# Windowed attention in an encoder layer: the second score product on all 128 rows of the array, and the products with v in alternating column halves

## The chip, the cores and the metric

The kernel runs on one core of a Trainium2 chip. The metric is device time in microseconds (us) of one execution of the whole kernel. PE is TensorE (PEld its weight loads), DVE is VectorE, ACT is ScalarE, POOL is GpSimd, SP is SyncE, which issues the DMAs.

## The reference, cut to what matters

The program is one hybrid encoder layer of 1024 tokens and 1024 features: a gated linear recurrence and a windowed attention side by side, a cross-attention into a memory, a gated MLP, each with its norm and residual. The change lies in the windowed attention alone: 8 query heads of 64 features share 2 key/value heads, and a token sees keys at a distance of at most 128. In blocks of 128 queries against up to three blocks of keys:

```python
    s = jnp.einsum('bnqhgd,bnkhd->bnhgqk', qb, kb).astype(jnp.float32) * (ATT_HEAD_DIM ** -0.5)
...
    s = jnp.where(valid[None, :, None, None], s, -jnp.inf)
    sk = sink.astype(jnp.float32).reshape(ATT_KV_HEADS, ATT_GROUP)[None, None, :, :, None, None]
    m = jnp.maximum(jnp.max(s, axis=-1, keepdims=True), sk)
    p = jnp.exp(s - m)
    p = p / (jnp.sum(p, axis=-1, keepdims=True) + jnp.exp(sk - m))
    o = jnp.einsum('bnhgqk,bnkhd->bnqhgd', p.astype(v.dtype), vb)
```

## The kernel before, in words

All engines work from instruction streams that are fixed when the program is built; each engine takes its own stream in order. A scheduler sorts the streams at build time, so that work of different parts is interleaved on PE: while the attention runs, the last chunks of the gate projections (`gate_chunk`, matmuls of L103 into `gate_ps`, 128x512 each) stand between its pieces.

Matrix products in full precision are made from a high and a low part of each operand (`_h`/`_l`, type float32r). For the scores the two parts of q are stacked: a tile `qs[h]` of 128 partitions holds the high part of head h in one half of the partitions and its low part in the other half (odd heads the other way round). `kh[g]` holds the high part of k in both halves, `kl[g]` its low part in both halves (`stacked`, L824 and after; the tiles come by DMA through two `stage` tiles, ACT writes the high parts and DVE the low ones).

The attention is a loop over 8 tiles `i` of 128 tokens and 2 groups `g` of 4 heads: 16 blocks, in the order (0,0), (0,1), (1,0) and so on. A block has two or three key tiles `ks` (two at both ends). Per block:

1. Scores, for each of the 4 heads: two matmuls into one PSUM bank `as` (three such banks): L863 multiplies the whole `qs` with `kh`, over all 128 rows of the array (128x384, or 128x256 at the ends); L865 multiplies the high half of `qs`, 64 rows, with the same half of `kl`.
2. DVE adds the band and takes the row maximum in one pass (L868, result `sm`), negates it (`nm`, L166), and ACT takes the exponentials with their sums (L879). DVE adds the sink's term and inverts (L881, L882), and scales the four heads (L166, `sm<-sm,den`).
3. PE transposes `sm` in pieces of 128x128, four heads into a bank `pt` (L889; two such banks); the middle key tile's bank is copied to `pT` by DVE (L891), the others by ACT (L893).
4. Products with v (L897): `po`, one bank, has 128 partitions, the first 64 for two of the heads (`par` 0) and the last 64 for the other two (`par` 1). The stationary operand is 64 columns wide, so that a product uses one half of the array's columns. In float32 one product is two matmul instructions in the trace. ACT copies `po` to `att` (L901).

The pool `pT` has two buffers, `sm` three, `ao` one. After the loop the attention's result is split (L914, L915) and multiplied with w_br (L103, `y`).

Of the kernel before, what the change touches and what calls it, by code (L numbers as in the profile page):

```python
# [52 lines left out]
def encoder_layer(ctx, tc, x, mem, positions, vecs, fin, sink, w_in, w_br, w_out, w_mq, w_mk, w_mv,  # L53
                  w_mo, w_up, w_down, ident_in, masks_in, band_in, invf_in, out):
    nc = tc.nc
# [39 lines left out]
    def proj_f(ps, w, act, kts=range(KT), koff=0, halves=(0, 1), width=512):  # L95
        """ps[c, tok] = w[k, c]^T act[k, tok] with weights stationary; act(kt, half) -> (hi, lo)."""
        wh, wl = w
        kts = list(kts)
        for n_, hf in enumerate(halves):
            n = 0  # L100
            for wx, ai in ((wh, 0), (wh, 1), (wl, 0)):
                for kt in kts:
                    nc.tensor.matmul(  # L103
                        ps[:, n_ * width:(n_ + 1) * width],
                        lhsT=wx[:, (kt + koff) * P:(kt + koff + 1) * P],
                        rhs=act(kt, hf)[ai],
                        start=(n == 0),
                        stop=(n == 3 * len(kts) - 1),
                    )
                    n += 1  # L110

# [7 lines left out]
    def hi_lo_cols(xs, k2, gcol, ps, hi, lo, w):  # L119
        """Feature chunks 2 k2, 2 k2 + 1 of the tiles xs, transposed, times the gain, as hi and lo."""  # L120
        for a in range(2):
            kt = 2 * k2 + a
            for j, t in enumerate(xs):
                nc.tensor.transpose(ps[:, a, j * P:(j + 1) * P], t[:, kt * P:(kt + 1) * P], ident)
        for a in range(2):
            kt = 2 * k2 + a
            g = vec[:, gcol + kt:gcol + kt + 1]
            nc.scalar.activation(hi[:, a, :], ps[:, a, :w], AF.Copy, scale=g)
            nc.vector.scalar_tensor_tensor(out=lo[:, a, :], in0=ps[:, a, :w], scalar=g,
                                           in1=hi[:, a, :].bitcast(F32),  # L130
                                           op0=ALU.mult, op1=ALU.subtract)

    def norm_half(src, gcol, xs_pool, name, alloc, hf, per=4):
        """Tiles src(hf * per ..) of [128, 1024] -> feature-major (hi, lo) lists of [128, 2, per * 128]."""
        xs = []
        for i in range(hf * per, (hf + 1) * per):
            t = src(i)
            s = xs_pool.tile([P, D], F32, tag="xs", name=f"{name}_xs{i}")
            ss = xs_pool.tile([P, 1], F32, tag="xss", name=f"{name}_ss{i}")
            rs = xs_pool.tile([P, 1], F32, tag="xrs", name=f"{name}_rs{i}")  # L140
            norm_stats(t, s, rs, ss)
            nc.vector.tensor_scalar(out=s, in0=t, scalar1=rs, scalar2=None, op0=ALU.mult)
            xs.append(s)
        w = per * P
        his, los = [], []
        for k2 in range(KT // 2):
            ps = work_psum(f"{name}_tp{hf}_{k2}")
            hi = alloc(f"{name}_h{hf}_{k2}", w)
            lo = alloc(f"{name}_l{hf}_{k2}", w)
            hi_lo_cols(xs, k2, gcol, ps, hi, lo, w)  # L150
            his.append(hi)
            los.append(lo)
        return his, los
# [17 lines left out]
    # With A the weights of two column chunks by halves of K, and B the normed input by halves of K and  # L171
    # of the tokens, the seven products are
    #   M1 = A11 B11, M2 = A12 B21, M3 = S4 B22, M4 = A22 T4, M5 = S1 T1, M6 = S2 T2, M7 = S3 T3.
# [21 lines left out]
    class Operand:  # L195
        """Half of the features by half of the tokens, as hi and lo."""
# [16 lines left out]
    class Strassen:  # L213
        """w_d: weights by column chunks; ts: the eight token tiles, which the norm overwrites; gcol: gains;
        tp: 12 tiles of operands; wq: weight sums; bf: four tiles of the norm's own."""
# [21 lines left out]
        def cols(self, hf, k2, dst):  # L237
            """Feature chunks 2 k2, 2 k2 + 1, transposed, times the gain."""
            for a in range(2):
                kt = 2 * k2 + a  # L240
                ps = self.bank(f"{self.nm}_tp{hf}{kt}")
                for j in range(4):
                    nc.tensor.transpose(ps[:, j * P:(j + 1) * P],
                                        self.ts[4 * hf + j][:, kt * P:(kt + 1) * P], ident)
                g = self.gcol + kt
                nc.scalar.activation(dst[:, a, :], ps, AF.Copy, scale=vec[:, g:g + 1])
# [9 lines left out]
        def half1(self, save12=None):  # L256
            """In steps, so that other work can come between."""
            nm, bf, ts = self.nm, self.bf, self.ts
# [48 lines left out]
        def work(self, tag, name, bufs, width=512):  # L307
            """The first chunks work in the tiles that the norm leaves behind, the others in a pool there."""
            if self.fp is None:
                n = self.used[tag] = self.used.get(tag, -1) + 1  # L310
                return self.left[tag][n % len(self.left[tag])]
            return self.fp.tile([P, width], F32, tag=tag, name=name, bufs=bufs)

        def pair(self, c, name, put):
            """put(row, half, in0, in1): the product of chunk c + row and token half is in0 + in1 (or in0)."""
# [37 lines left out]
        def into(self, outs, tag, names, bufs):  # L353
            """A put that writes the products to tiles of its own."""
            def put(r, hf, a, b):
                if r not in outs:
                    outs[r] = self.work(tag, names[r], bufs, S)
                o = outs[r][:, hf * 512:(hf + 1) * 512]
                if b is None:
                    nc.scalar.copy(o, a)  # L360
                else:
                    add(o, a, b)
            return put

    # ================= token mixing =================
# [19 lines left out]
    # The first chunks' products are plain float32 ones, whose operands need no splitting.  # L385
    w_first, n_plain = [], 2
    for i in range(NT):
        if i < n_plain:
            w = npool.tile([P, 1024], F32, tag="n", name=f"wk{i}")
# [6 lines left out]
    # The memory's norm: its gains go into the operand, its row scales into the products.  # L396
# [73 lines left out]
    # forget-gate bounds: f = fs * tanh(z / 2) + fb  # L470
# [132 lines left out]
    # The weights of the output and the down-projection, in the same form with the even and the odd chunks as  # L603
    # the halves of K; their sums by halves of the columns: T1 T3 T4 T2.
# [47 lines left out]
    with ExitStack() as gla:  # L652
# [10 lines left out]
        def gla_head(h, finish_last):  # L663
# [25 lines left out]
            # same-token terms  # L689
# [34 lines left out]
            # states between tiles  # L724
# [41 lines left out]
            # per-head RMSNorm, output gate  # L766
# [56 lines left out]
    # Stacked operands: a head's q is [hi; lo] (odd heads [lo; hi]) against [k_hi; k_hi], plus hi with k_lo.  # L823
# [24 lines left out]
    for i in range(NT):  # L848
# [4 lines left out]
        for g in range(2):  # L853
# [3 lines left out]
            for pr in range(2):  # L857
                for a in range(2):
                    ps = one_bank(f"as{u}_{pr}", "as", 3, 512)
                    h = 4 * g + 2 * pr + a  # L860
                    rows = HA if h % 2 == 0 else HB
# [3 lines left out]
                    nc.tensor.matmul(ps[:, :nk], lhsT=qs[h][rows, tok], rhs=kl[g][rows, kr],  # L865
# [29 lines left out]
            for par in range(2):  # L895
                for a, j in enumerate(ks):
# [33 lines left out]
    # Left operands of the output projection, by halves of the tokens.  # L930
# [49 lines left out]
    def out_proj(w_d, tag, act, hf, psum4, emit, nk=KT):  # L980
        """Half the tokens times w, by column halves, as the weights arrive: ps[tok, c] = act^T w."""
# [25 lines left out]
    def token_product(name, nk, left, right, banks, first, put, tail, hook=None):  # L1007
        """A product of a left operand (tokens) and a right one (columns) of nk chunks each, in four banks."""
# [69 lines left out]
    # ================= memory cross-attention =================  # L1078
# [8 lines left out]
    def hl(name, tag, bufs, src, scale=None):  # L1087
        """Exact high and low parts of [128, 1024] src (times a power of two)."""
# [90 lines left out]
    # ================= channel mixing =================  # L1179
# [27 lines left out]
    # The left operands, by halves of the tokens: A11 S3 A12 A22 S1 S2 S4.  # L1207
# [53 lines left out]
    def emit_out(i, part):  # L1261
        """Column half part of the residual is complete; the row is when part ends it."""
# [122 lines left out]
```

## Time and profile before

| | |
|---|---|
| Runs of the kernel before | 1803.36, 1806.0, 1807.61 us; median 1806.0 us |
| Profiled execution, from first to last instruction | 1803.6 us (no other time of it is listed) |
| Its PE busy | 1763.9 us (98%) |
| Its DVE, ACT busy | 1195.2 us (66%), 756.5 us (42%) |
| Granted clock of PE, mean | 0.998 of full speed |
| The attention's loop, first score matmul to last product | about 588 to 730 us of the span |

The page shows one execution. Busy times of PE contain modelled ends: a matmul counts as busy until its last result is out, while the next one has long begun, so a full row of "busy" doesn't say that PE is at its peak. Starts are measured; the distance from one start to the next is what an instruction costs the engine. In the chain of waits, a piece's time is its share of the way to the end.

### The profile page before, as it was taken

The page shows a single profiled execution, that of the slowest core. Times are in us where ns is not written, and L with a number is a line of the kernel's source. Part 1 is how long each engine was busy: PE and PEld are TensorE (multiplying, and loading weights), DVE is VectorE, ACT ScalarE, POOL GpSimd, SP SyncE. Part 2 cuts the span into 40 slices and gives each one's busy share as a digit, 9 for nine tenths or more (in the row PEclk, how much of TensorE's full clock was granted, in tenths as well). Part 3 has the DMA queues.
Part 4 walks back from the last instruction along what each step waited for, and adds up shares of the span by engine and source line. Part 5 has one row for each costly group of instructions (what it writes and reads, how often), then busy time and mean ns, then how long its engine had stood idle before and what let it go on. Part 6 is the DMA issues. An engine that isn't in the chain of part 4 may idle for free.

```text
span 1803.6 us, 21596 instructions
## 1 busy us (share of the span) xinstructions
PE 1763.9 (98%) x8372; PEld 1419.8 (79%) x8372; DVE 1195.2 (66%) x1692; ACT 756.5 (42%) x1128; POOL 33.9 (2%) x45
## 2 busy tenths in 40 slices
PE   8999999999999999999999999999999999999998
PEld 7678878888888755788778887878888888788886
DVE  5877765488884576676577454788676677656544
ACT  6643333333232455432344334544433344425335
POOL 1000000000000000000000000000000000000001
PEclk9999999999999999999999999999999999999999
DMA  8375652622213511245267213322223322486663
GB/s 293 130 245 184 208 182 99 257 76 106 94 47 121 164 36 47 94 143 203 88 248 264 70 47 117 117 88 100 99 88 131 109 88 100 153 295 221 206 191 135
DMA packets 85207, 256.37 MB, mean 142 GB/s; under 512 B 8912, under 2 KB 9296, under 8 KB 85104
## 3 DMA queue, kind: packets, MB, share of 16 engines
q1 hardware_dynamic: 85104, 254.99, 41.4%
q8 instruction: 66, 1.08, 0.2%
q14 instruction: 37, 0.30, 0.1%
HBM read 182.73 MB, written 71.57 MB: 141 GB/s over the span
## 4 chain that ended last, share of the span: by engine, by line
PE 77%; DVE 10%; DMA 7%; issue 2%; ACT 2%; POOL 1%; SPq 0%; POOLq 0%; ACTq 0%; DVEq 0%
PE gate_ps L103 6%; PE dnX L1026 5%; PE y L103 5%; PE mq L993 4%; PE xq_ps L103 3%; PE dnZ L1026 3%; PE moX L1026 2%; PE sc L710 2%; PE ao L897 2%; DMA hr<-hid_d 2%; PE moZ L1026 1%; PE xo L1157 1%; PE as L865 1%; PE pt L889 1%; PE xs L1131 1%
## 5 line engine op out<-in xcount | busy, mean ns | idle before, releaser
L103 PE MATMUL gate_ps<-n1B,wh 128*128 128x512 f32 x512 | 135.6, 401 | 0.0
L92 DVE TENSOR_TENSOR wl<-wr,wh 128x1024 fp32r<-128x1024 f32 x70 | 85.4, 1223 | 54.8 <-ACT wh L91 24.1
L91 ACT CAST wh<-wr 128x1024 fp32r<-128x1024 f32 x70 | 73.6, 1052 | 103.1 <-PE xq_ps L103 22.0
L103 PEld LDWEIGHTS gate_ps<-n1B,wh 128*128 128x128 f32 x512 | 93.5, 188 | 21.5 <-issue 4.0
L177 DVE TENSOR_TENSOR hl<-hr,hh 128x1024 fp32r<-128x1024 f32 (+1 forms) x42 | 47.6, 1134 | 48.5 <-ACT hh L1286 48.2
L1286 ACT CAST hh<-hr 128x1024 fp32r<-128x1024 f32 (+1 forms) x42 | 41.0, 976 | 79.9 <-DMA hr<-hid_d 38.2
L103 PE MATMUL gate_ps<-n1B,wl 128*128 128x512 f32 x256 | 69.6, 400 | 0.0
L710 PE MATMUL sc<-Z,kc 128*128 128x128 f32 x448 | 61.4, 288 | 2.2 <-DVE Z L716 2.0
L710 PEld LDWEIGHTS sc<-Z,kc 128*128 128x128 f32 x448 | 56.4, 192 | 8.8 <-issue 7.2
L868 DVE CUSTOM_DVE_ANT_0 sm<-as,band,sink_t 128x384 f32<-128x384 f32 (+1 forms) x64 | 36.9, 581 | 30.7 <-PE as L865 29.3
L103 PEld LDWEIGHTS gate_ps<-n1B,wl 128*128 128x128 f32 x256 | 47.3, 188 | 10.6 <-issue 1.1
L993 PE MATMUL mq<-wh,xoh 128*128 128x512 f32 x128 | 50.6, 397 | 2.1 <-DVE h L1053 1.3
L993 PE MATMUL mq<-wl,xoh 128*128 128x512 f32 x128 | 50.8, 397 | 0.0
L993 PE MATMUL mq<-wh,xol 128*128 128x512 f32 x128 | 50.3, 394 | 0.0
L705 ACT COPY kc<-KZ 128x512 f32<-128x512 f32 x28 | 17.9, 638 | 76.0 <-DVE KZ L719 54.9
L649 ACT ACTIVATE gate<-gate_ps 128x512 f32<-128x512 f32 x32 | 19.2, 599 | 65.8 <-PE gate_ps L103 61.5
L713 DVE COPY_PREDICATED A<-masks,sc 128x1024 f32<-128x1024 uint32 x28 | 38.2, 1364 | 10.5 <-PE sc L710 10.5
L879 ACT ACTIVATE sm<-sm,nm 128x384 f32<-128x384 f32 (+1 forms) x64 | 37.2, 583 | 5.2 <-DVE nm L166 4.9
L719 DVE TENSOR_TENSOR KZ<-KZ,F 128x1024 f32<-128x1024 f32 x28 | 34.5, 1231 | 1.9 <-ACT kc L706 1.0
L103 PE MATMUL xq_ps<-n_l,wh 128*128 128x512 f32 x128 | 34.5, 397 | 0.0
L897 PE MATMUL ao<-pT,vaT 128*64 128x256 f32 x176 | 34.5, 391 | 0.0
L716 DVE TENSOR_TENSOR Z<-Z,F 128x1024 f32<-128x1024 f32 x28 | 34.3, 1224 | 0.0
(1858 smaller groups left out, 4685.5 us busy)
## 6 DMA issues: line engine op xcount, KB each, us to landing
hr<-hid_d SPq DMA_DIRECT2D x35, 512.0 KB
ws<-in_w_down SPq DMA_DIRECT2D x22, 512.0 KB
td_d<-ws SPq DMA_DIRECT2D x22, 512.0 KB
hid_d<-gc SPq DMA_DIRECT2D x20, 512.0 KB
pj_d<-pj SPq DMA_DIRECT2D x18, 512.0 KB
wr<-in_w_in SPq DMA_DIRECT2D x16, 512.0 KB
gate_d<-gate SPq DMA_DIRECT2D x16, 512.0 KB
wr<-in_w_mq SPq DMA_DIRECT2D x16, 512.0 KB
```

What stands on the lines that cost most here:

```text
L91: nc.scalar.copy(h, r)
L92: nc.vector.tensor_tensor(out=l, in0=r, in1=h.bitcast(F32), op=ALU.subtract)
L103: nc.tensor.matmul(ps[:, n_ * width:(n_ + 1) * width], lhsT=wx[:, (kt + koff) * P:(kt + koff + 1) * P], rhs=act(kt, hf)[ai], start=(n == 0 ...
L177: nc.vector.tensor_tensor(out=o, in0=a, in1=b, op=ALU.subtract)
L710: nc.tensor.matmul(flat(ps)[:, js], lhsT=kc[:, js], rhs=raw(Zf, [[2 * b, 64 // b], [S + b, 2], [1, b]], j * P), start=True, stop=True)
L713: nc.vector.copy_predicated(A, masks[:, li].unsqueeze(1).broadcast_to([P, NT, P]), flat(ps).rearrange("p (a b) -> p a b", b=P))
L868: nc.vector.tensor_tensor_reduce(out=sm[:, hh, :nk], in0=ps[:, :nk], in1=flat(band)[:, m0:m0 + nk], scale=1.0, scalar=sink_t[:, 4 * g + hh ...
L879: nc.scalar.activation(sm[:, h, :nk], sm[:, h, :nk], AF.Exp, bias=nm[:, h:h + 1], accum_out=den[:, h:h + 1])
L897: nc.tensor.matmul(po[par * 64:(par + 1) * 64, :], lhsT=vaT[:, j, g * 64:(g + 1) * 64], rhs=pT[:, a, par * 256:(par + 1) * 256], start=(a ...
L993: nc.tensor.matmul(tiles[j], lhsT=x_, rhs=w[wx][:, a * 512:(a + 1) * 512], start=(k == 0 and n == 0), stop=(k == nk - 1 and n == 2))
L1026: nc.tensor.matmul(banks[j], lhsT=av[ai][:, q, j * P:(j + 1) * P], rhs=bv[bi][:, q, :], start=(first and k == 0 and n == 0), stop=(k == nk ...
L1286: nc.scalar.copy(hi[:, :n], r[:, :n])
```

## The change

The second score matmul takes all 128 rows of `qs` and `kl`; its sum then holds the product of the two low parts as well, which was left out before. The loop over the products with v is turned inside out: the key tile is the outer loop, the half of the columns the inner one. (The rest of the diff removes comments and doc strings or leaves blank lines in their place. A line that was added above shifts L824 to L860 by one.)

```diff
-                    rows = HA if h % 2 == 0 else HB
                     kr = slice(k0, k0 + nk)
                     nc.tensor.matmul(ps[:, :nk], lhsT=qs[h][:, tok], rhs=kh[g][:, kr],
                                      start=True, stop=False)
-                    nc.tensor.matmul(ps[:, :nk], lhsT=qs[h][rows, tok], rhs=kl[g][rows, kr],
+                    nc.tensor.matmul(ps[:, :nk], lhsT=qs[h][:, tok], rhs=kl[g][:, kr],
                                      start=False, stop=True)
...
             po = one_bank(f"ao{u}", "ao", 1, 256)
-            for par in range(2):
-                for a, j in enumerate(ks):
+            for a, j in enumerate(ks):
+                for par in range(2):
                     nc.tensor.matmul(po[par * 64:(par + 1) * 64, :],
                                      lhsT=vaT[:, j, g * 64:(g + 1) * 64],
                                      rhs=pT[:, a, par * 256:(par + 1) * 256],
                                      start=(a == 0), stop=(a == len(ks) - 1))
```

On PE's stream, at the end of block 3 (token tile 1, second group; `ao_1`, with the first scores of token tile 3, `as_0_0`), a count of x2 is two products, not two instructions of the trace:

```order
 L863 MATMUL as_0_0_4627<-kh_4201,qs_4203 128x384
 L889 MATMUL pt_1_2_4489<-ident,sm_1_4442 128x128 x4
-L897 MATMUL ao_1_4495<-pT_1_4476,vaT 64x256 x2
+L897 MATMUL ao_1_4495<-pT_1_4476,vaT 64x256 x6
 L865 MATMUL as_0_0_4627<-kl_4202,qs_4203 128x384
-L897 MATMUL ao_1_4495<-pT_1_4476,vaT 64x256 x4
 L863 MATMUL as_0_0_4631<-kh_4201,qs_4204 128x384
 L865 MATMUL as_0_0_4631<-kl_4202,qs_4204 128x384
```

The six products, two of one column half and four after the score matmul before, now stand together, ahead of it, in alternating halves.

The same stream one block later (token tile 2, first group; `ao_0`):

```order
 L889 MATMUL pt_0_2_4550<-ident,sm_0_4503 128x128 x4
-L897 MATMUL ao_0_4556<-pT_0_4537,vaT 64x256 x2
+L897 MATMUL ao_0_4556<-pT_0_4537,vaT 64x256 x4
 L863 MATMUL as_1_0_4688<-kh_4213,qs_4215 128x384
 L865 MATMUL as_1_0_4688<-kl_4214,qs_4215 128x384
-L897 MATMUL ao_0_4556<-pT_0_4537,vaT 64x256 x4
+L897 MATMUL ao_0_4556<-pT_0_4537,vaT 64x256 x2
 L863 MATMUL as_1_0_4692<-kh_4213,qs_4216 128x384
```

Here four products come ahead of the score matmuls instead of two: the first two key tiles for both halves; the third key tile's two products follow. Over the whole loop the 88 products stand in 24 runs instead of 25, and of the 64 matmuls of L865 ten had a product as direct neighbour before, and nine now. The streams of DVE, ACT, POOL and SP keep their instructions and their order.

## Rows read from the trace of the kernel before

**Rows 1.** The page: busy time of the engines, and PE's clock in 40 slices.
```profile
PE 1763.9 (98%) x8372; PEld 1419.8 (79%) x8372; DVE 1195.2 (66%) x1692; ACT 756.5 (42%) x1128; POOL 33.9 (2%) x45
...
PEclk9999999999999999999999999999999999999999
```

**Rows 2.** Windows: the loop's four stretches, busy us of each engine.
```profile
588.00:626.00 38.00, 38.00 (x166) 28.46 (x164) 19.05 (x34) 17.19 (x28) 0.00 (x0) 1.00 0.66 194
626.00:642.00 16.00, 16.00 (x69) 9.40 (x68) 11.43 (x45) 9.98 (x31) 0.00 (x0) 1.00 0.01 1
642.00:721.40 79.40, 79.39 (x381) 47.22 (x379) 52.68 (x195) 45.24 (x134) 0.00 (x0) 1.00 0.14 47
721.40:731.00 9.60, 9.60 (x57) 6.43 (x57) 4.19 (x15) 5.11 (x16) 0.00 (x0) 1.00 0.15 48
```

**Rows 3.** Who waited for whom, 588 to 731: us in total, times, longest.
```profile
DVE sm L868 <- PE as L865: 29.3, 27, 2.8
...
ACT att L901 <- PE ao L897: 20.3, 16, 2.9
DVE pT L891 <- PE pt L889: 18.4, 15, 2.6
```

**Rows 4.** The chain in order of time: start us, us, what.
```profile
570.38 17.96 PE gate_ps L103 x79
...
638.57 1.02 PE ao L897 x8
...
642.22 2.19 PE ao L897 x12
644.41 0.37 PE as L865
644.78 0.38 PE as L863
...
648.11 0.43 PE gate_ps L103
648.54 0.17 PE as L863
648.71 0.44 PE pt L889 x4
649.15 1.01 PE ao L897 x4
650.15 0.37 PE as L865
650.53 1.45 PE ao L897 x8
...
666.03 0.57 PE ao L897 x2
```

**Rows 5.** Windows: matmuls of L865 alone (PE, PEld), same four stretches.
```profile
588.00:626.00 38.00, 2.89 (x8) 1.46 (x8) 1.00 0.66 194
626.00:642.00 16.00, 5.42 (x13) 2.19 (x12) 1.00 0.01 1
642.00:721.40 79.40, 18.84 (x44) 8.04 (x44) 1.00 0.14 47
```

**Rows 6.** Timeline 622 to 626: the last piece of q, and its matmul.
```profile
623.00 1.21 DVE L829 SCALAR_TENSOR_TENSOR qs<-stage,qs 64x1024 fp32r<-64x1024 f32 x1
...
625.57 0.28 PE L863 MATMUL as<-kh,qs 128*128 128x256 f32 x1
```

**Rows 7.** Timeline, block 8: scaling, transposes, copy.
```profile
683.90 1.40 DVE L166 TENSOR_SCALAR sm<-sm,den 128x384 f32<-128x384 f32 x4
...
686.43 0.82 PE L889 MATMUL pt<-ident,sm 128*128 128x128 f32 x6
...
687.29 0.69 DVE L891 COPY pT<-pt 128x512 f32<-128x512 f32 x1 [1.25 <-PE pt L889]
```

**Rows 8.** Windows at the start and the end of the span: PE busy, granted clock.
```profile
0.00:10.00 10.00, 4.34 (x18) 3.89 (x19) 1.55 (x11) 3.39 (x8) 0.20 (x4) 1.00 0.79 279
...
1780.00:1803.60 23.60, 15.75 (x70) 12.71 (x68) 6.78 (x18) 8.86 (x17) 2.19 (x4) 0.94 0.24 90
```

## The prediction

> **What bounds the kernel now.** The page comes first: PE is busy for 1763.9 of 1803.6 us, and its granted clock stands at full speed in every slice [rows 1]. So the kernel is PE's, and what an edit on PE's stream is worth depends on whether PE is also the last to finish in the stretch where the edit lies. The windows over the attention's loop answer that: from 588 to 731 us PE shows no idle time, while DVE and ACT are busy for about half of the first stretch and two thirds of the others [rows 2]. The waits agree: the long ones are DVE's and ACT's for PE, 29.3 us for scores, 18.4 us for transposes, 20.3 us for products with v [rows 3]. But "busy" holds modelled ends, so the price of an instruction has to be read from the chain in order of time, where a piece's time is what it adds to the way to the end [rows 4]. What the reader should see there: a score matmul L863 of 384 columns costs 0.17 us where the matmuls behind it are transposes, which use the whole array as it does, and 0.37 us where its neighbours are matmuls of L865; an L865, with the same columns on 64 rows, costs 0.37 us everywhere. Twice as much for the same columns: the array is not working in that time.
>
> **The second score matmul.** I read the difference, 0.37 - 0.17 = 0.20 us, as the price of going from matmuls on one set of rows to matmuls on another, since it is paid once into an L865 and once out of it (0.37 for L865, 0.37 for the L863 behind it) [rows 4]. There are 64 of them, so 128 changes. Ten have a product with v as neighbour; those products use another shape of the array, and the change from full rows to that shape stays. That leaves 118 x 0.20 = 23.6 us of PE's time. By stretch, from the counts of L865 (8, 12 and 44, counting weight loads) [rows 5]: 16 changes, 3.2 us, in the first; 24, 4.8 us, in the second; 78, 15.6 us, in the third. The new rows themselves cost nothing: L863 takes all 128 rows, and its 0.17 us is the price of 384 columns. The same operands are read; no wait is added.
>
> **The products with v.** Four matmuls of one column half cost 1.01 us; eight that have both halves in hand cost 1.02 us at 638.57 us [rows 4]. So two halves do run at the same time, at full rate, when PE has both in its queue. Elsewhere it hasn't: the old order puts all of half 0 ahead of half 1, and half 0's last key tile waits for a copy of pT, with half 1 stuck behind it. Eight in the mixture 2 + 6 cost 1.45 us, which is six places of 0.22 us instead of four; twelve cost 2.19 us. In alternating order n matmuls need n/2 places: 1.02 us for eight, 1.45 us for twelve, and about 0.58 us for four (two in one half cost 0.57 us) [rows 4]. In the chain over the loop there are four runs of twelve (2.19 to 1.45 us, 0.74 each), six blocks with runs of four and eight (2.46 to 1.60 us, 0.86 each), and two with runs of two and ten (0.57 + 1.45 to 1.60 us, 0.42 each): 3.0 + 5.2 + 0.8 = 9.0 us, all in the third stretch. The four blocks at the loop's ends, whose runs stand between gate matmuls or are paired already, give about 1 us, half in the first stretch and half in the last.
>
> **What of it reaches the end.** PE alone would thus be quicker by 3.2 + 0.5, 4.8, 15.6 + 9.0 and 0.5 us, 33.6 us in sum. In the third stretch that leaves PE 79.4 - 24.6 = 54.8 us of work, against 52.7 us of DVE [rows 2]. The cover is gone: DVE's work was hidden under PE's, and now the two are level, in streams that keep their order. So late next are DVE's results. Two bounds: if DVE never waits, PE's 54.8 us hold; if it goes on waiting as it does now, far less comes out. The wait that can't all go is that of the copy pT: DVE scales a block, PE transposes it, and DVE copies the middle piece. In block 8 scaling ends at 685.30 us and the copy starts at 687.29 us, with 1.25 us of idle DVE before it, and little on PE between the two is touched by the change [rows 7]. Over the loop these waits are 18.4 us in 15, 1.2 us each [rows 3]. For the eleven blocks of the third stretch I keep half of it, 0.6 us each, since score maxima can fill the other half: 52.7 + 6.6 = 59.3 us, 20.1 us saved (bounds 24.6, and 7 if the whole 1.2 us and as much as half of it again in waits for scores stay: 52.7 + 13.2 + 6.6 = 72.5 us). In the second stretch PE's 11.2 us are level with DVE's 11.4 us [rows 2]: I take 12.0, 4.0 us saved (between 2.5 and 4.6). In the first, the last piece of q is ready at 624.21 us and its matmul starts at 625.57 us, 1.36 us later [rows 6]; if q's pieces, which come by DMA, are not earlier, only 1.4 us can be gained there, else 3.7 us; I take 2.4. With 0.5 us at the end: 2.4 + 4.0 + 20.1 + 0.5 = 27.0 us. What follows the loop starts earlier by as much; it hangs on the last att and is bound by PE. The profiled execution, 1803.6 us, would become 1776.6 us; the median of the runs is 2.4 us above it, so 1779.0 us.
>
> **The rivals.** *PE stays the bound throughout.* All 33.6 us come out: 1772.4 us. For it speaks that DVE's 52.7 us are still below PE's 54.8; against it that both would have to run without a gap in streams that wait for each other. Chance 0.10.
>
> *DVE and the waits around it bind harder.* The lower bounds, 1.4 + 2.5 + 7 + 0.5 = 11.4 us, give 1794.6 us; the case reaches up to some 20 us saved, 1786 us. For it: fifteen waits for transposes and 27 for scores now [rows 3], and orders that were not made for the new pace. Against it: most of these waits exist because PE is slow. Chance 0.12.
>
> *The halves do not overlap when they alternate*, because the weights of one half wait for the matmul of the other. Then the products cost what they cost now, PE keeps 79.4 - 15.6 = 63.8 us in the third stretch, above DVE's 59.3, and 2.4 + 4.0 + 15.6 = 22.0 us are saved: 1784 us. The eight in 1.02 us speak against it, though there the pairs were found by PE, not written so [rows 4]. Chance 0.04. The Trainium skill, "TensorE: Matmul & The Clock Gate", Part 3, "What overlaps and what doesn't", states this rule: a weight load overlaps matmuls in flight only where their row groups differ, and matmuls start and end strictly in program order. Both halves here use the same rows, so by it the alternation would give nothing; in this trace eight matmuls fit into the time of four, which the rule would not allow.
>
> *PE's clock falls.* With PE waiting for DVE in the third stretch, the granted clock could go from 2.4 to 1.2 GHz there, and its 54.8 us of work would cost up to twice as much: 54.8 - 27.0 = 27.8 us slower, 1834 us. It decides against the change once about 27 us of PE's work run at the lower level. At the end of the span, with 15.75 us busy of 23.6, the mean was 0.94; but in the first 10 us, with 4.34 busy, it was 1.00 [rows 8], and the loop would leave PE busy for nine tenths. Chance 0.03.
>
> *The change doesn't do what it says*: the 0.20 us hang on something other than rows, on adding into a bank just written, say, and the halves don't pair either. Then 1806 us. Against it: 79 gate matmuls of 512 columns, which add into one bank, cost 17.96 us, 0.23 each, and one behind an L865 0.43, 0.20 more [rows 4]. Chance 0.02.
>
> **The numbers.** The likeliest case has 0.69; its own range is 20 to 32 us saved, 1774 to 1786 us. For 8 in 10, I take in PE's bound and the upper half of DVE's: 1771 to 1790 us. A measurement of this kernel can tell about 0.2%, 3.6 us, from no change. Faster by more: 0.69 + 0.10 + 0.12 + 0.04 = 0.95; within it 0.02; slower 0.03.
>
> **What would show it.** L865 at 0.17 us in the chain and no price around it; runs of products at 1.02 and 1.45 us for eight and twelve; PE with idle time in the third stretch, ended by DVE's scaling, copies and maxima, and DVE busy there for about nine tenths. Wrong would be L865 still at 0.37 us, PE without idle time in the third stretch (then all 33.6 us come out), or DVE's waits for transposes as long as now. A loop that is shorter by 27 us with a total that isn't would mean that a later stage, fed by DMA, took the time back.

## The result, and the profile after

The changed kernel takes 1772.1 us (median of 4 runs, 1771.2 to 1773.9), the kernel before 1804.7 us (median of 4, one of them new): a ratio of 0.982, 95% interval 0.980 to 0.984. That is 32.6 us less; 27.0 were forecast. The profiled execution has a span of 1771.0 us.

The page of the changed kernel, busy times of the engines, and the clock:

```profile
PE 1731.9 (98%) x8372; PEld 1412.5 (80%) x8372; DVE 1193.4 (67%) x1692; ACT 755.7 (43%) x1128; POOL 33.9 (2%) x45
...
PEclk9999999999999999999999999999999999999999
```

PE lost 32 us of busy time with the same number of instructions, its weight loads 7, the other engines less than 2 each, and the clock stays full [rows 1]. The windows of the loop's four stretches, cut at the same places of the work (the first score matmul, block 2's first score matmul, the copies to att of block 2 and of block 13, the last copy to att); columns are us of the stretch, then busy us (instructions) of PE, PEld, DVE, ACT, POOL, clock, DMA:

```profile
585.83:620.33 34.50, 34.50 (x165) 27.74 (x164) 19.06 (x34) 17.14 (x28) 0.00 (x0) 1.00 0.72 214
620.33:633.66 13.33, 13.33 (x83) 10.46 (x82) 12.50 (x52) 10.97 (x34) 0.00 (x0) 1.00 0.00 1
633.66:690.46 56.80, 56.76 (x382) 40.55 (x381) 51.36 (x191) 44.90 (x140) 0.00 (x0) 1.00 0.20 66
690.46:696.57 6.11, 6.11 (x42) 3.96 (x41) 2.87 (x8) 2.90 (x10) 0.00 (x0) 1.00 0.09 17
```

Between the same marks the kernel before took 37.9, 18.4, 79.3 and 6.8 us (in [rows 2] the cuts are rounded). So the loop gained 3.4 + 5.0 + 22.5 + 0.7 = 31.6 us, and PE's row still shows next to no idle time in all four. The rest of the 32.6 us of the two spans lies outside: the loop starts 2.4 us earlier and what follows it takes 1.3 us more. No work there was changed, and in the profiles of all the runs below the loop starts anywhere between 584.2 and 589.1 us.

The chain in order of time in the third stretch:

```profile
636.85 1.45 PE ao L897 x12
638.29 0.37 PE as L865
638.67 0.18 PE as L863
638.84 0.17 PE as L865
...
641.97 0.44 PE pt L889 x4
642.41 1.01 PE ao L897 x8
643.42 0.37 PE as L863
643.79 0.18 PE as L865
643.97 0.58 PE ao L897 x4
```

L865 costs 0.17 to 0.18 us wherever its neighbours use the whole array, against 0.37 before [rows 4]; the first score matmul behind a run of products still costs 0.37, whichever of the two it is. Twelve matmuls of the products cost 1.45 us, eight 1.01, four 0.58: the forecast values to 0.01 us. The waits of the other engines from the loop's start to its end:

```profile
DVE sm L868 <- PE as L865: 13.9, 14, 1.9
...
ACT att L901 <- PE ao L897: 7.5, 8, 2.1
ACT sm L879 <- DVE nm L166: 5.0, 5, 2.3
DVE pT L891 <- PE pt L889: 4.9, 9, 1.3
```

VectorE's wait for the transposes fell from 18.4 us to 4.9 [rows 3]. I had kept half of it. PE's own list of waits has one entry, behind the loop and the same in both kernels:

```profile
PE y L103 <- ACT gate L649: 0.7, 1, 0.7
```

A wait that is hidden by modelled ends doesn't show there, but it can in the list of the weight loads (PEld). The entry that grew most is that of loads for transposes which wait for ACT's copy out of a bank `pt`; before and after:

```profile
PEld pt L889 <- ACT pT L893: 0.7, 2, 0.4
```

```profile
PEld pt L889 <- ACT pT L893: 1.8, 6, 0.4
```

### The profile page after: what moved, and what is told of

The parts are those of the page before. It is cut to its first block, busy times and chain, and to the rows that moved or that the text cites. A ratio compares the mean times of both kernels' runs of the same rounds, so it can differ in the third digit from the quotient of the medians.

```text
span 1771.0 us, 21596 instructions
## 1 busy us (share of the span) xinstructions
PE 1731.9 (98%) x8372; PEld 1412.5 (80%) x8372; DVE 1193.4 (67%) x1692; ACT 755.7 (43%) x1128; POOL 33.9 (2%) x45
## 4 chain that ended last, share of the span: by engine, by line
PE 79%; DVE 9%; DMA 6%; ACT 2%; issue 2%; POOL 1%; SPq 0%; POOLq 0%; ACTq 0%; DVEq 0%
PE dnX L1026 6%; PE gate_ps L103 6%; PE dnZ L1026 5%; PE y L103 5%; PE mq L993 4%; PE xq_ps L103 3%; PE sc L710 2%; PE moX L1026 2%; PE moZ L1026 1%; PE xo L1157 1%; PE ao L897 1%; PE pt L889 1%; PE xs L1131 1%; DMA F<-pj_d 1%; DVE wl L92 1%
## 5 line engine op out<-in xcount | busy, mean ns | idle before, releaser
L103 PEld LDWEIGHTS gate_ps<-n1B,wh 128*128 128x128 f32 x512 | 93.8, 189 | 18.4 <-issue 1.5
L103 PE MATMUL xq_ps<-n_h,wh 128*128 128x512 f32 x128 | 33.1, 395 | 0.0
```

The lines of the kernel that those rows point to most:

```text
L103: nc.tensor.matmul(ps[:, n_ * width:(n_ + 1) * width], lhsT=wx[:, (kt + koff) * P:(kt + koff + 1) * P], rhs=act(kt, hf)[ai], start=(n == 0 ...
```

## The experiments

After the result my theory was: each change of shape between neighbouring matmuls costs PE about 0.2 us, the halves of the columns overlap fully, and VectorE's waits take a little back. The rivals: VectorE's waits take much back, and a smaller or dearer price of the shapes explains the rest; the halves don't overlap; it is matmuls on 64 rows that are slow, not the change to them. In the table the loop runs from the first score matmul to the last copy to att, and "to y" to the first matmul of the stage behind it, "through y" to the start of that stage's last matmul, in the profiled execution of each kernel, in us. In the last five rows the scheduler moved gate matmuls into the loop or out of it, and with fewer of them behind the loop the first matmuls of y wait for `att_h`; so "through y" is the one to compare.

| kernel | runs of the comparison: ratio to before, 95% interval | loop | to y | through y |
|---|---|---|---|---|
| before | | 142.3 | 146.1 | 233.1 |
| changed | 0.982 (0.980 to 0.984) | 110.7 | 114.5 | 201.5 |
| rows alone | 0.988 (0.985 to 0.991) | 121.0 | 124.9 | 211.8 |
| halves alone | 0.995 (0.992 to 0.997) | 132.2 | 136.0 | 223.0 |
| both score matmuls on 64 rows | 0.995 (0.993 to 0.997) | 134.4 | 138.2 | 225.2 |
| last key tile first | 0.981 (0.978 to 0.984) | 110.3 | 112.3 | 200.8 |
| all copies on ACT | 0.982 (0.979 to 0.984) | 111.1 | 116.0 | 203.0 |
| some more for VectorE | 0.986 (0.983 to 0.989) | 116.4 | 117.8 | 207.3 |
| more for VectorE | 0.988 (0.985 to 0.991) | 121.5 | 122.9 | 211.5 |

**The rows alone, on the kernel before.**

```diff
-                    nc.tensor.matmul(ps[:, :nk], lhsT=qs[h][rows, tok], rhs=kl[g][rows, kr],
+                    nc.tensor.matmul(ps[:, :nk], lhsT=qs[h][:, tok], rhs=kl[g][:, kr],
```

> The kernel before with the row part of the change alone: L865 on all 128 rows, the products with v in their old order. My theory (0.20 us for each change of PE between matmuls of different shape): 118 of 168 changes go, 23.6 us off PE, and nearly all of it off the time, since the change as a whole gave back only some 2 us to waits: 22 to 24 us less than before, L865 at 0.17 to 0.18 us in the chain. The rival, that VectorE's waits take half of a gain in the third stretch: 14 to 18 us less.

Measured: 1784.7 us against 1805.2 in the same comparison, 20.5 us less; the loop 21.3 us shorter. The chain (this file's lines are one lower: L862 and L864 are the two score matmuls, L896 the products):

```profile
644.96 1.01 PE ao L896 x4
645.96 0.37 PE as L862
646.33 0.17 PE as L864
646.50 1.45 PE ao L896 x8
647.95 0.37 PE as L862
648.32 0.18 PE as L864
648.50 0.17 PE as L862
```

The score matmuls behave as expected and the products cost what they cost before. The gain is 2 us under the sum, above all that the rival allows. So the loss of 2 us is there already while VectorE has 10 us more room than in the changed kernel, which speaks against VectorE's waits as its cause. The sum below finds a third of it in the price and the rest in short gaps ahead of transposes.

**The halves alone, on the kernel before.**

```diff
-            for par in range(2):
-                for a, j in enumerate(ks):
+            for a, j in enumerate(ks):
+                for par in range(2):
```

> The kernel before with the other part alone: the products with v in alternating halves, L865 on 64 rows. My theory (halves overlap fully): 9 to 10 us less than before, runs of eight in 1.02 and of twelve in 1.45 us. The rival (weights of one half wait for matmuls of the other): no change, runs of eight at 1.7 us or more. If the two parts add, this run and the rows alone give the 32 us of both together; if VectorE binds once both are in, their sum is above it.

Measured: 1794.3 us, 10.9 less than 1805.2; the loop 10.05 us shorter. The chain:

```profile
644.74 0.43 PE gate_ps L103
645.17 0.17 PE as L863
645.35 0.44 PE pt L889 x4
645.79 1.45 PE ao L897 x12
647.23 0.37 PE as L865
```

Twelve in 1.45 us: the halves overlap. And the two parts add: 21.3 + 10.05 = 31.3 us of the loop, 31.6 for both together. A second bound behind PE would have taken something from the sum; nothing was taken.

**What the price hangs on: both score matmuls on 64 rows, on the kernel before** (it leaves out the product of q's low part with k's high part).

```diff
-                    nc.tensor.matmul(ps[:, :nk], lhsT=qs[h][:, tok], rhs=kh[g][:, kr],
+                    nc.tensor.matmul(ps[:, :nk], lhsT=qs[h][rows, tok], rhs=kh[g][rows, kr],
```

> The kernel before with the first score matmul, L863, on 64 rows too, the same half as L865; it leaves out the product of q's low part with k's high part. It tells what the 0.20 us hang on. If on a change of shape between neighbours: L865 behind L863 costs 0.17 us, changes of shape fall from 168 to 137, and the time falls by about 6 us (31 x 0.20). If on a matmul of 64 rows itself (filling half an array costs as much more): 64 more such matmuls at 0.2 to 0.4 us each, 13 to 25 us slower.

Measured: 1796.1 us, 9.1 less, with 64 more matmuls on half of the rows. The chain and, behind it, the timeline of the same kernel:

```profile
648.88 0.37 PE as L863
649.25 0.17 PE as L865
649.43 0.43 PE gate_ps L103
```

```profile
646.84 0.44 PE L865 MATMUL as<-kl,qs 64*128 64x384 f32 x1
646.85 0.44 PE L863 MATMUL as<-kh,qs 64*128 64x384 f32 x1
647.22 0.87 PE L889 MATMUL pt<-ident,sm 128*128 128x128 f32 x6
```

L865 behind an L863 of its own shape costs 0.17 us, and it adds into the bank that this L863 has just written. So it is the change that costs, not the 64 rows, nor the adding. The gain is above the 6 us expected, because of something that I had not thought of: where a score matmul of one head meets one of the next, on the other half of the rows, both start within 0.01 us and run together (here L865 and L863). The trace of the loop has 20 such pairs, one of them 0.05 us apart; at 0.17 us each they are worth 3.4 us. (The way through y shows 8.0 us and not 9.1: five gate matmuls, 1.1 us, that stood ahead of the loop before stand in it here.)

**Fewer runs of products: the last key tile first, on the changed kernel.**

```diff
-            for a, j in enumerate(ks):
+            for a, j in reversed(list(enumerate(ks))):
...
-                                     start=(a == 0), stop=(a == len(ks) - 1))
+                                     start=(a == len(ks) - 1), stop=(a == 0))
```

> The changed kernel, with the key tiles of the products with v taken last first: the piece of pT that is copied last comes first, so that a block's products wait once and stand in one run, 16 runs instead of 24, 32 changes of shape instead of 48. My theory: 16 x 0.17 us, 2.8 us less than the changed kernel (which was 32.5 us below the kernel before), so 35 us below before. Rival: the later start of the products delays the copies to att and the blocks behind them, and PE waits for what it saves: no difference from the changed kernel, or 1 to 3 us slower than it.

Measured: 1772.1 us, ratio 0.981, the same as the changed kernel's within the intervals. The profile shows 2.3 us less on the way to y, near the 2.8 expected, but only 0.7 us less on the way through y, and the runs can't tell that from none. What is missing is in waits. The chain now holds ACT's copy ahead of some of the transposes, and eight of the twelve gate matmuls behind the loop have moved into it, so that the first matmuls of y wait for `att_h`.

```profile
640.58 0.45 PE pt L889 x4
641.11 0.59 ACT pT L893
641.70 0.04 issue
641.75 0.66 PE pt L889 x4
```

So neither side is refuted: the changes of shape that go are worth about what they were taken for, and most of it turns into waits.

**Is VectorE a bound of the changed kernel? All copies of transposes on ACT.**

```diff
-                if a == 1:
-                    nc.vector.tensor_copy(pT[:, a, :], pt)
-                else:
-                    nc.scalar.copy(pT[:, a, :], pt)
+                nc.scalar.copy(pT[:, a, :], pt)
```

> The changed kernel with every copy of transposes to pT on ACT: VectorE has 16 x 0.69 = 11 us less to do in the loop, ACT as much more. If PE alone bounds the loop, as the sums over the changed kernel say now (of 110.6 us from the first score matmul to the last product, column time and changes of shape leave about nothing to waits): no gain, 54 changes of shape instead of 48 cost 1.1 us, loop 111 to 112 us. If VectorE, at 90% in the third stretch, holds PE up as I forecast: 2 to 5 us less.

Measured: 1772.1 us, the same as the changed kernel. Its third stretch, between the same marks:

```profile
632.20:689.25 57.05, 57.00 (x376) 39.23 (x377) 45.27 (x181) 49.78 (x150) 0.00 (x0) 1.00 0.20 66
```

VectorE has 6.1 us less to do in it, and it takes 57.05 us instead of 56.8, with three gate matmuls fewer; the way through y is 1.4 us longer, of which six more changes of shape explain about 1. Taking work from VectorE is worth nothing. This run alone doesn't show that PE is the only bound, since ACT has as much more to do; the sum of PE's distances below says it more directly.

**Giving VectorE more**, by a second copy of the same piece to pT, in the blocks of the first group or in all.

```diff
                     nc.vector.tensor_copy(pT[:, a, :], pt)
+                    if g == 0:
+                        nc.vector.tensor_copy(pT[:, a, :], pt)
```

> The changed kernel with VectorE's copy to pT made twice in every other block (the first group): some 0.6 us of idle work for VectorE in 8 blocks, 3.6 us of it in the third stretch, which then needs 55.0 us of VectorE in 56.8. If VectorE's remaining room can be used: no more than the 4 more changes of shape, 0.7 us, loop 111 to 112 us. If waits already bind it, the 3.6 to 4.8 us show in full.

> The changed kernel with VectorE's copy to pT made twice in every block: 9.6 us of idle work in the loop, 6.6 us in the third stretch, 58.0 us of VectorE against 56.8. VectorE must now bind there. If it can run without gaps, the loop grows by some 1.2 us and the 8 more changes of shape, 1.5 us: about 113 us. If the streams' order leaves it the gaps that I forecast for the changed kernel, 0.6 us a block: 65 us for the third stretch, loop 119 us.

(In the second of them the copy stands without its condition.) Measured: 1781.0 and 1783.9 us, 8.9 and 11.7 above the changed kernel's median, of which the way from the first score matmul through y shows 5.8 and 10.0 us. The rest of the difference lies outside this way, where nothing was changed. It goes with the granted clock, though no run shows that this is the cause: three of the four runs of the second kernel have a mean granted clock of 0.995, those of the changed kernel 0.998 or 0.999, and of the kernel before the runs at 0.994 and 0.995 in the comparison of the first three experiments took 1812 and 1809 us, those at 0.998 1802 to 1805. In the third stretch of the two kernels, which holds 17 gate matmuls (3.9 us) more than that of the changed kernel:

```profile
636.80:697.30 60.50, 60.45 (x397) 43.39 (x398) 52.45 (x195) 46.80 (x142) 0.00 (x0) 1.00 0.18 62
```

```profile
634.04:698.60 64.56, 62.24 (x396) 42.80 (x397) 56.53 (x198) 45.67 (x135) 0.00 (x0) 1.00 0.22 74
```

Neither is what "room that can be used" would give. The second copies take 0.69 us each: with 11.0 us more for VectorE 10.0 us show, and PE for the first time has idle time in that stretch, 2.3 us; with half as much work 5.8 us show. PE's own list now has waits inside the loop, 1.9 us in the first kernel and 4.9 us in the second; the longest of each:

```profile
PE ao L899 <- DVE pT L893: 1.4, 1, 1.4
```

```profile
PE pt L889 <- DVE sm L166: 2.3, 3, 1.1
```

So the changed kernel seems to stand near the point where VectorE takes over: less for it gains nothing, more costs nearly its full time. That is argued, not shown. The second copy stands between the transposes and the products, and delays these even where VectorE has room; and in both kernels all gate matmuls behind the loop have moved into it, so that y waits for `att_h`. These runs don't separate the three.

## Why the prediction was right, and where not

**The price of a change of shape: right, but not all of it came out.** The loop can be added up from what each matmul adds on PE. In the middle of its own kind a score matmul of 384 columns adds 0.173 us, one of 256 0.117, a transpose 0.109 and a gate matmul 0.227: 81.3 us for 96, 32, 176 and 184 of them in both kernels. The runs of products (first start to last start, and one place of 0.216 us) take 30.4 us before and 20.4 us after. Of the whole, 142.2 and 110.6 us to the last product, 30.5 and 8.9 us are left, for 168 and 48 changes, 0.18 us each on average. But the average mixes three things. Added up one by one, by the distances of ends as in the chain, a change between full rows and 64 rows costs 0.195 us into L865 and 0.192 out of it on average. The changes at the runs of products, which stay, are cheaper, 0.145 us into a run and 0.185 out of it on average. (Of the price into a run, 0.05 us lies within the run's time above.) And the gaps between matmuls of one shape grew from 0.8 to 2.4 us, most of it in a few gaps of 0.1 to 0.3 us ahead of transposes, where by their list the loads wait for ACT's copies; with the rows alone they are 2.4 us as well. So the term of 23.6 us came to 21.3, by the loop of the rows alone: the 118 changes were worth 22.8, and 1.5 us came back in gaps that the forecast didn't have.

**The products: right.** Forecast about 10.0 us in all, 10.0 measured by the runs above, 10.05 by the loop of the halves alone. The rule of the Trainium skill that was set against it ("TensorE: Matmul & The Clock Gate", Part 3, "What overlaps and what doesn't"), that a weight load overlaps matmuls in flight only where the row groups differ, does not hold here: eight matmuls on the same rows and in alternating halves fit into 1.01 us, as four do.

**What of it reaches the end: wrong.** "For the eleven blocks of the third stretch I keep half of it, 0.6 us each": that term, 6.6 us of VectorE's waits on top of 52.7 us, which made the stretch 59.3 us long, is the step that failed. The stretch took 56.8 us. In the whole loop the gaps on PE that the shapes don't explain grew by only 1.5 us, and by the list of the weight loads the waits that grew are for ACT, above all for its copies, not for VectorE. VectorE worked 51.4 of the 56.8 us; it was still idle for 5.4, but PE set the time. Its waits for transposes shrank with PE's work, because they were the picture of a VectorE that was ahead, not a part of the way to the end; I named this argument against the lower bound and didn't let it count for the middle. So the rival "PE stays the bound throughout" is what happened, at 1772.4 us forecast and 1772.1 measured; the likeliest case, 1774 to 1786 us, is missed by 2 us, while the wider 1771 to 1790 us holds it. That the rival fits to 0.3 us is luck in part: the loop gave 31.6 of its 33.6 us, and 1.0 us came from outside the loop, where nothing was changed. The second stretch gained 5.0 us, more than the 4.0 taken, and the first 3.4 instead of 2.4: q's last piece came earlier too, 33.1 us after the loop's start instead of 36.0.

**The other rivals.** The clock stayed at full speed; with some 5 us more work for VectorE the loop is longer by about as much, as the last two experiments show, so the case that it binds harder may have been nearer than the result says. That the price hangs on adding into a bank just written is refuted by L865 at 0.17 us. One of the prediction's own signs was wrong (idle time of PE in the third stretch), and of VectorE's waits for transposes about a quarter stayed, not half; the sign that it gave for the opposite, PE without idle time there, is the one that came.

## What to carry to other kernels

Where matmuls of different shapes (rows or columns of the array) alternate, read from the chain what one adds with and without a neighbour of another shape: here a change to 64 rows or back costs 0.19 us, more than 384 columns (0.173), so filling unused rows with a product that nobody needs was cheaper than leaving them out. Two halves of the array ran at the same time here where both stood in PE's stream ahead of the next wait; write them alternately. Waits of an engine that is ahead are no forecast of what it will cost when it is level: compare its busy time with what the bounding engine will have left. Here 51.4 us of work against 56.8 cost nothing, and a few microseconds more may have been enough to cost.

## What the runs showed of the hardware that I had not expected

Two matmuls of 64 rows each, on different halves of the rows and into different banks, started 0.01 us apart and both took 0.44 us, without anything being written for it; one loop had 20 such pairs. And two engines with 51.4 and 56.8 us of interleaved work ran with hardly a gap on the slower one, in streams with fixed order.
